# Softmax minus one-hot over 8192 columns: half of the loads and stores of X issued on Pool's queue in place of SP's

## The chip, the cores and the metric

The kernel runs on one core of a Trainium2 chip. The metric is device time in microseconds (us), the median of three runs; lower is better. The engines are named as in the profile: DVE is VectorE, ACT is ScalarE, POOL is GpSimd (called Pool here), SP is SyncE, which does nothing but issue transfers, and PE is TensorE.

## What is computed

The reference takes logits of shape 8 x 1024 x 8192 in fp32 and one integer label for each of the 8192 rows. For each row it computes the softmax and subtracts 1 at the label's column:

```
logits_max = np.max(logits, axis=-1, keepdims=True)
exp_logits = np.exp(logits - logits_max)
softmax = exp_logits / np.sum(exp_logits, axis=-1, keepdims=True)
one_hot[batch_idx, seq_idx, labels] = 1.0
return (softmax - one_hot).astype(np.float32)
```

268 MB are read and 268 MB are written.

## The kernel before

**Blocks and slots.** The 8192 rows are cut into B = 32 blocks of 256 rows. A block lies in SBUF as 128 partitions with G = 2 rows each (j = 0 and 1), so that partition p holds 64 KB that are contiguous in HBM. The tile X has SLOTS = 3 such blocks, and block b uses slot b % 3. Everything is done in place: a block is loaded into X, computed on in X, and stored from X. Block b + 3 can be loaded only when block b has been stored.

**Pieces.** Each load and each store of a block is made in two pieces of 4.19 MB, q = 0 and 1. PIECES (line 105) knows two ways to cut. In "r", piece q is row j = q of all 128 partitions. In "h", piece q is both rows of the even (q = 0) or the odd (q = 1) partitions. LOADS and STORES (lines 13 and 14) say which cut each block uses: blocks 0 to 3 and 31 are loaded by rows, the others by halves; block b is stored as block b + 3 is loaded. So a load's piece q overlaps only the piece q of the store before it in the same slot.

**Order of the transfers.** `transfers` (lines 139 to 144) is written out by hand: the six loads of blocks 0 to 2, and then for each block b its two stores and the two loads of block b + 3. All are issued on SP's queue in this order. `run` (line 63) records an instruction; where it must wait for a semaphore, the engine that issues it waits, and whatever stands behind it on that engine waits too. `load` (line 120) waits for the store of the same piece three blocks earlier to have landed (semaphores `put`). The load of block 2's second row waits for `w_iota`, since the iota is made in that place of X first. `store` (line 130) waits for the VectorE instruction that finishes the piece's last row: for a store by halves that is row 1 of the block, for both halves.

**Compute.** For each of the 64 row tiles (128 x 8192): VectorE takes the negated maximum (`row_max`, line 155, TENSOR_REDUCE), ScalarE computes exp with the row's sum, VectorE takes the reciprocal, ScalarE scales by it, and VectorE computes x - (iota == label) (SCALAR_TENSOR_TENSOR). On VectorE the maximum of row tile t + 1 stands ahead of the last step of row tile t. The iota lies in PSUM as int16. It is made once, on Pool (line 86), and copied to PSUM by VectorE (line 98). The maximum of a row tile waits for all pieces that hold a part of it: by halves, for both loads of the block.

**Pool** makes an identity for the transpose of the labels, then the iota, and after that has nothing to do. All instructions go through `run`, so the profile gives line 68 for nearly all of them; they are told apart by tile and operation. Line 198 is SP's wait for the last stores.

Of the kernel before, what the change touches and what calls it, by code (L numbers as in the profile page):

```python
# [8 lines left out]
G = 2  # L9
SLOTS = 3  # L10
# [7 lines left out]
def kernel(  # L18
# [6 lines left out]
    nc = tc.nc  # L25
# [30 lines left out]
    with tc.tile_critical():  # L56
        sem = tc.alloc_semaphore
        got = [[sem(f"got{i}{q}") for q in range(2)] for i in range(SLOTS)]
        put = [[sem(f"put{i}{q}") for q in range(2)] for i in range(SLOTS)]
# [3 lines left out]
        def run(engine, waits, counter, method, **operands):  # L63

            waits = list(dict.fromkeys(waits))
            for w in waits[:-1]:
                engine.wait_ge(*w)  # L67
            instruction = getattr(engine, method)(**operands)  # L68
            for w in waits[-1:]:
                instruction._wait_ge(*w)  # L70
            step = 16 if method == "dma_start" else 1
            instruction.then_inc(counter, step)
            count[counter.name] = count.get(counter.name, 0) + step
            return counter, count[counter.name]
# [3 lines left out]
        w = run(nc.gpsimd, [], pool, "memset", ap=ident[:], constant=0.0)  # L78
# [13 lines left out]
        for j in range(G):  # L92
            w = run(
                nc.tensor, [w_ident, w_lab], pe, "transpose",
                out=lab_ps[:, j, :], in_=lab_f[:, j, :], identity=ident[:],
            )
# [14 lines left out]
        def meets(a, b):  # L111

            sets = [[set(range(*d.indices(n))) for d, n in zip(p, (P, G))] for p in (a, b)]
            return all(x & y for x, y in zip(*sets))


        loaded, stored, finished = {}, {}, []
        last_made = [((every, slice(G - 1, G)), w_iota)]

        def load(b, q):  # L120
            piece = PIECES[LOADS[b]][q]
            ps, js = piece
            before = stored.get(b - SLOTS, last_made if b == SLOTS - 1 else [])
            w = run(
                nc.sync, [w for other, w in before if meets(piece, other)], got[b % SLOTS][q],
                "dma_start", out=X[ps, b % SLOTS, js, :], in_=x_b[b, ps, js, :],
            )
            loaded.setdefault(b, []).append((piece, w))

        def store(b, q):  # L130
            piece = PIECES[STORES[b]][q]
            ps, js = piece
            w = run(
                nc.sync, [finished[b * G + js.stop - 1]], put[b % SLOTS][q],
                "dma_start", out=o_b[b, ps, js, :], in_=X[ps, b % SLOTS, js, :],
            )
            stored.setdefault(b, []).append((piece, w))

        transfers = [(load, b, q) for b in range(SLOTS) for q in range(G)]
        for b in range(B):  # L140
            transfers += [(store, b, q) for q in range(G)]
            if b + SLOTS < B:
                transfers += [(load, b + SLOTS, q) for q in range(G)]
# [23 lines left out]
        for t in range(T):  # L167
            x = row(t)
            label = lab[:, t % G, t // G : t // G + 1]
            w = run(  # L170
                nc.scalar, [w_max], act, "activation",
                out=x, in_=x, func=Act.Exp, bias=m[:, t : t + 1], scale=1.0, accum_out=s[:, t : t + 1],
            )
# [13 lines left out]
            for c, w in zip(cols, scaled):  # L187
                w = run(
                    nc.vector, [w], dve, "scalar_tensor_tensor",
                    out=x[:, c], in0=iota[:, c], scalar=label, in1=x[:, c],  # L190
                    op0=Alu.is_equal, op1=Alu.subtract, reverse1=True,
                )
# [36 lines left out]
```

## Time and profile before

| | |
|---|---|
| median of 3 runs | 1251.36 us (1250.57 to 1251.69) |
| the profiled execution | 1251.85 us |
| its span in the profile | 1250.1 us |
| DVE busy | 1116.5 us (89%) |
| ACT busy | 919.0 us (74%) |
| POOL busy | 7.4 us (1%) |
| moved | 536.99 MB, 430 GB/s over the span |
| issues of X on SP's queue | 64 loads, 64 stores |
| median from issue to landing, by halves | 19.3 us a load, 28.9 us a store |

The rows of the page that name an operation read: line, engine, operation, output<-input, shapes, count, busy us in all, mean ns of one, then the engine's idle time just ahead of them and what ended it. A DMA queue's row gives packets, MB, and the time of its packets as a share of 16 engines' span. In the chain and in the timeline the first number is the start and the second the duration, both in us from the start of the span; "x2" is two instructions merged into one row, so that its duration includes what lies between them. SPq is SP issuing a transfer; the transfer itself goes on long after the issue has ended, until its landing, when the last of its bytes is reported by semaphore.

### The profile page before, as it was taken

The page shows a single profiled execution, that of the slowest core. Times are in us where ns is not written, and L with a number is a line of the kernel's source. Part 1 is how long each engine was busy: PE and PEld are TensorE (multiplying, and loading weights), DVE is VectorE, ACT ScalarE, POOL GpSimd, SP SyncE. Part 2 cuts the span into 40 slices and gives each one's busy share as a digit, 9 for nine tenths or more (in the row PEclk, how much of TensorE's full clock was granted, in tenths as well). Part 3 has the DMA queues.
Part 4 walks back from the last instruction along what each step waited for, and adds up shares of the span by engine and source line. Part 5 has one row for each costly group of instructions (what it writes and reads, how often), then busy time and mean ns, then how long its engine had stood idle before and what let it go on. Part 6 is the DMA issues. An engine that isn't in the chain of part 4 may idle for free.

```text
span 1250.1 us, 646 instructions
## 1 busy us (share of the span) xinstructions
PE 0.4 (0%) x2; PEld 0.3 (0%) x2; DVE 1116.5 (89%) x196; ACT 919.0 (74%) x194; POOL 7.4 (1%) x7
## 2 busy tenths in 40 slices
PE   0000000000000000000000000000000000000000
PEld 0000000000000000000000000000000000000000
DVE  5999999988899888998888988889888898888993
ACT  3888888777777777777778777687767877778782
POOL 2000000000000000000000000000000000000000
DMA  9999999999999999999999999999999999999998
GB/s 405 419 432 424 432 434 436 434 430 424 428 430 436 436 432 436 434 432 436 436 436 434 432 432 430 430 428 436 432 436 436 436 436 436 434 436 419 447 417 350
DMA packets 11317, 536.99 MB, mean 430 GB/s; under 512 B 2064, under 2 KB 2064, under 8 KB 2096
## 3 DMA queue, kind: packets, MB, share of 16 engines
q1 hardware_dynamic: 11264, 536.88, 99.6%
q10 hardware_dynamic: 48, 0.07, 0.0%
q14 instruction: 5, 0.04, 0.0%
HBM read 268.50 MB, written 268.44 MB: 430 GB/s over the span
## 4 chain that ended last, share of the span: by engine, by line
DMA 74%; DVE 21%; SPq 2%; ACT 1%; issue 1%; PE 0%; ACTq 0%; DVEq 0%
DMA out_dram<-X 72%; DVE m L68 10%; DVE X L68 10%; SPq L68 2%; DMA X<-in_logits_dram 2%; ACT X L68 1%; DMA lab_raw<-in_labels_dram 1%; DVE iota L68 0%; DVE r L68 0%; DVE lab_f L68 0%; PE iota L68 0%; DVE lab L68 0%; ACTq L224 0%; DVEq L67 0%; SPq L56 0%
## 5 line engine op out<-in xcount | busy, mean ns | idle before, releaser
L68 DVE TENSOR_REDUCE m<-X 128x1 f32<-128x8192 f32 x64 | 555.2, 8675 | 98.3 <-DMA X<-in_logits_dram 98.3
L68 ACT ACTIVATE X<-X,m 128x8192 f32<-128x8192 f32 x64 | 455.8, 7122 | 212.6 <-DVE m L68 212.6
L68 DVE SCALAR_TENSOR_TENSOR X<-iota,lab,X 128x8192 f32<-128x8192 int16 (+1 forms) x65 | 559.6, 8611 | 3.8 <-ACT X L68 3.8
L68 ACT ACTIVATE X<-X,r 128x8192 f32<-128x8192 f32 (+1 forms) x65 | 456.0, 7017 | 95.6 <-DVE r L68 95.6
L68 DVE RECIPROCAL r<-s 128x1 f32<-128x1 f32 x64 | 9.8, 154 | 7.3 <-ACT X L68 7.3
L68 ACT ACTIVATION_READ_ACCUMULATOR X<-X,m 128x1 f32 x64 | 11.9, 186 | 0.0
L68 DVE CAST lab_f<-lab_raw 32x256 f32<-32x256 int32 x1 | 1.0, 993 | 7.4 <-DMA lab_raw<-in_labels_dram 7.4
L68 POOL IOTA X<- 128x8192 int16 x1 | 6.9, 6943 | 0.0
L68 DVE TENSOR_SCALAR iota<-X 128x4096 int32<-128x4096 int32 x1 | 4.4, 4427 | 0.1
L68 ACT ACT_TABLE_LOAD x1 | 1.3, 1283 | 1.4 <-SPq L56 1.4
L68 DVE COPY lab<-iota 128x64 f32<-128x64 f32 x1 | 0.2, 225 | 0.5 <-PE iota L68 0.5
L68 PE MATMUL iota<-ident,lab_f 32*128 32x32 f32 x2 | 0.4, 302 | 8.5 <-DVE lab_f L68 8.5
L68 PEld LDWEIGHTS iota<-ident,lab_f 32*128 32x128 f32 x2 | 0.3, 196 | 8.4 <-DVE lab_f L68 8.4
L68 POOL TENSOR_SCALAR_AFFINE_SELECT ident<-ident 32x32 f32<-32x32 f32 x1 | 0.2, 202 | 0.1
L68 POOL MEMSET ident<- 32x32 f32 x1 | 0.1, 114 | 0.5 <-SPq L56 0.5
L213 POOL MEMSET const-bfloat16-1.0<- 128x1 bf16 x1 | 0.1, 106 | 0.0
L213 POOL MEMSET const-uint8-127<- 128x1 uint8 x1 | 0.1, 106 | 0.0
L213 POOL MEMSET const-float32-0.0<- 128x1 f32 x1 | 0.1, 103 | 0.2 <-issue 0.2
L213 POOL MEMSET const-float32-1.0<- 128x1 f32 x1 | 0.1, 103 | 0.0
## 6 DMA issues: line engine op xcount, KB each, us to landing
X<-in_logits_dram SPq DMA_DIRECT2D x10, 4096.0 KB, 20.6
out_dram<-X SPq DMA_DIRECT2D x6, 4096.0 KB, 21.9
out_dram<-X SPq DMA_DIRECT2D x58, 28.9
X<-in_logits_dram SPq DMA_DIRECT2D x54, 19.3
lab_raw<-in_labels_dram ACTq DMA_DIRECT2D x1, 64.0 KB, 6.5
```

The lines of the kernel that those rows point to most:

```text
L68: instruction = getattr(engine, method)(**operands)
L213: nc = _bacc.Bacc("TRN2", target_bir_lowering=False, num_devices=1)
```

## The change

A list of the two issuing engines is added, and each load and store takes its engine from it by its piece number q:

```
         loaded, stored, finished = {}, {}, []
+        ring = [nc.sync, nc.gpsimd]
...
             w = run(
-                nc.sync, [w for other, w in before if meets(piece, other)], got[b % SLOTS][q],
+                ring[q], [w for other, w in before if meets(piece, other)], got[b % SLOTS][q],
                 "dma_start", out=X[ps, b % SLOTS, js, :], in_=x_b[b, ps, js, :],
             )
...
             w = run(
-                nc.sync, [finished[b * G + js.stop - 1]], put[b % SLOTS][q],
+                ring[q], [finished[b * G + js.stop - 1]], put[b % SLOTS][q],
                 "dma_start", out=o_b[b, ps, js, :], in_=X[ps, b % SLOTS, js, :],
             )
```

Piece 0 (row 0, or the even partitions) stays on SP's queue, and piece 1 (row 1, or the odd partitions) goes to Pool's queue. Each of the two queues keeps the order of its own pieces; between the two there is no order but the semaphores that were there before. The slots, the pieces, the waits and all instructions of the other engines stay. The wait for the last stores stays on SP.

More of the change, by code (lines that the diff above doesn't have):

```diff
@@ L117 @@
         loaded, stored, finished = {}, {}, []
+        ring = [nc.sync, nc.gpsimd]
         last_made = [((every, slice(G - 1, G)), w_iota)]
@@ L124, in load @@
             w = run(
-                nc.sync, [w for other, w in before if meets(piece, other)], got[b % SLOTS][q],
+                ring[q], [w for other, w in before if meets(piece, other)], got[b % SLOTS][q],
                 "dma_start", out=X[ps, b % SLOTS, js, :], in_=x_b[b, ps, js, :],
@@ L133, in store @@
             w = run(
-                nc.sync, [finished[b * G + js.stop - 1]], put[b % SLOTS][q],
+                ring[q], [finished[b * G + js.stop - 1]], put[b % SLOTS][q],
                 "dma_start", out=o_b[b, ps, js, :], in_=X[ps, b % SLOTS, js, :],
```

## The prediction

> **What bounds the kernel now.** I read the page first: busy shares, the DMA rows, the chain's shares, the costliest groups.
>
> ```profile
> PE 0.4 (0%) x2; PEld 0.3 (0%) x2; DVE 1116.5 (89%) x196; ACT 919.0 (74%) x194; POOL 7.4 (1%) x7
> ...
> q1 hardware_dynamic: 11264, 536.88, 99.6%
> ...
> DMA 74%; DVE 21%; SPq 2%; ACT 1%; issue 1%; PE 0%; ACTq 0%; DVEq 0%
> ...
> L68 DVE TENSOR_REDUCE m<-X 128x1 f32<-128x8192 f32 x64 | 555.2, 8675 | 98.3 <-DMA X<-in_logits_dram 98.3
> ```
>
> The 16 DMA engines are the bound: one queue, q1, which is SP's, keeps them busy 99.6% of the span, and VectorE's idle time ahead of the row maximum is all put down to loads. Pool is almost unused. Then the chain of waits in order of time, at the last steady blocks and the end:
>
> ```profile
> 1056.46 37.44 DMA out_dram<-X
> 1094.47 0.60 SPq L68
> 1095.11 37.43 DMA out_dram<-X
> 1132.55 19.28 DMA X<-in_logits_dram
> 1151.86 8.69 DVE m L68
> ```
>
> (The short rows of issue lie between them.) One store follows another at 1095.11 - 1056.46 = 38.65 us. A block moves four pieces of 4.19 MB, two loads and two stores, so one piece takes **D = 9.66 us**, and all 128 take 1237 us of the 1250.1 us span. From 1151.86 on, the chain is VectorE's to the end. Third, SP's own queue in the timeline, which shows how the order covers its waits:
>
> ```profile
> 1094.47 1.23 SPq L68 DMA_DIRECT2D out_dram<-X  x2
> 1122.90 10.16 SPq L68 DMA_DIRECT2D X<-in_logits_dram  x2
> 1133.11 1.06 SPq L68 DMA_DIRECT2D out_dram<-X  x2
> ```
>
> Two stores are issued; 28.4 us later the first has landed and SP issues the first load; the second store lands 10 us later, then the second load and at once the next two stores. While SP waits for the first store, the second is still moving. That is why the engines never run dry. Last, the view of the tile X and the start of the timeline:
>
> ```profile
> L68 SPq DMA_DIRECT2D X<-in_logits_dram x64: 328/507/531, 1.0 to 1171.3; - x64
> L68 SPq DMA_DIRECT2D out_dram<-X x64: 343/595/802, 47.0 to 1233.9; - x64
> DMA to landing us min/median/max: 12.4/20.7/49.4
> ```
>
> ```profile
> 0.96 13.07 SPq L68 DMA_DIRECT2D X<-in_logits_dram  x6
> 1.31 6.94 POOL L68 IOTA X<- 128x8192 int16 x1
> 13.58 8.68 DVE L68 TENSOR_REDUCE m<-X 128x1 f32<-128x8192 f32 x1
> ```
>
> The quickest transfer needs 12.4 us from issue to landing and 9.66 of them are data, so a queue that has run dry loses **G = 2.8 us** between the last byte of one transfer and the first byte of the next (issue, way out, way back of the semaphore; I take half of it on either side).
>
> **The change part by part.** In the built program the lists of TensorE, VectorE and ScalarE are the same. Of SP's 128 transfers of X, 64 go to Pool, behind its iota, in the same order. Nothing is removed: the bytes are the same, and q1 is already at 99.6%, so the data terms cannot shrink. SP's issue time (0.5 to 0.6 us each) was hidden and is worth nothing. What changes is **what covers a wait**. Each queue now runs store, wait for its landing, load, next store. A load waits behind a store of its own queue, and only the other queue can cover these 2.8 us.
>
> Take both queues to share the engines evenly. If both stores of a block start together, they land together, and each block leaves the engines idle for 2.8 us. If Pool's queue has w us of work left when SP's store lands, only 2.8 - w is idle. They do start together: at 98.91 SP issues both stores of block 1 within 1.2 us, because one VectorE result releases both. From then on w changes per block by the difference in turnaround between the two queues, **d**.
>
> d is not in this trace. Pool issues no DMA there. The nearest rows are SP's issues, 0.33 to 0.80 us; below, Pool could save such an issue (d = -0.5, which makes SP the lagging queue at the same price); above, the longest Pool row is the iota, 6.9 us, far from anything like an issue. I take **d = 0.6**, one more SP issue.
>
> - Start. Pool's loads begin behind the iota, which ends at 1.31 + 6.94 = 8.25, so with 1.4 + 0.6 their data from 10.25. Row 0's load, alone so far, has about 1.8 us left (landed about 13.4, less 1.4) and takes twice that. The row maximum, at 13.58 just behind it, comes **1.7 us** later, and VectorE is the chain until 203 us.
> - Early blocks. 2.8 - 0.6n for n = 1 to 4: 2.2 + 1.6 + 1.0 + 0.4 = **5.2 us**.
> - Middle. With w between 2.8 and about one piece, nothing is idle.
> - Late blocks. w cannot grow past a piece: a store needs the row after its block to have been reduced (order of VectorE), so it is ready 8.67 + 8.74 = 17.4 us after both halves of the next block's load. Then SP's queue waits for Pool's load through VectorE, is empty itself, and Pool's own turnaround is bare. From about 16 blocks of 0.6 on (block 18), some 13 blocks lose between 0 and 2.8 each. I take 0.6, what Pool lags by each time: **8 us**.
> - End. Before, the last waited-for load landed at 1151.84; the VectorE chain from there to the last store's issue (1233.9) is 82.1, and a transfer at least 12.4, in all 94.5; the ten pieces left then were 96.6. The two are nearly even. If Pool's half of that load comes w = 9 us later while SP works ahead, the chain sets the end: 9 - 2.1 = **6.9 us**.
>
> Sum 1.7 + 5.2 + 8 + 6.9 = 21.8 us. The profiled execution took 1251.85 (span 1250.1 and 1.75 around it); with the sum 1273.7. The median shown is 0.5 lower, 1251.36; so **1273 us**, +1.7%. The last three terms all have the cover as their reason: without any of it they would be 81 us.
>
> VectorE's large instructions all run at one rate: 8192 elements in 8675 ns (maximum) and 8742 ns (last step), 4096 in 4427 ns (copy of the iota), 1.06 to 1.08 ns each; none shows a faster mode. The Trainium skill, SBUF — State Buffer, "SBUF: two separate sides", warns against exactly this move: while VectorE holds the port pair that it shares with GpSimd in a two-port mode, GpSimd can't write descriptors, and Pool's DMAs starve. Its condition is not met by these rows as I read them; were it met, each Pool issue could wait one VectorE instruction, an estimate of up to 8.7 us x 29 blocks = 252 us. The same skill, DMA: Bandwidth & Descriptors, "Issuing engines are not separate DMA queues", says that several issuers save sequencer time only; by it alone the sum would be 0. No run here shows either for Pool.
>
> **Rivals.**
> 1. *A bare turnaround in every block.* Two ways lead there: d about 0, so that the queues stay in step; or the engines do not share evenly between the queues, so that the favoured one always finishes, waits for VectorE, and leaves the other's turnaround uncovered. 29 loads wait for a store: 29 x 2.8 = 81 us, 1332; with the longer turnaround of 3.4, 99 us, 1350. For it: both stores of a block have one releaser. Against it: any steady difference d takes the queues apart.
> 2. *All covered.* If one queue lags from the first by 3 to 9 us (Pool's loads start 7.3 us after SP's) and stays so, the start's 1.7 and an end between 0 and 3 remain, and the late start may be hidden: 1250 to 1255. Against it: the common release at 98.9 puts them in step.
> 3. *Faster.* Not every block takes 38.65 us: from 241.23 to 785.91 the chain's 14 blocks take 38.91 on average, 3.6 us too many in all. If that is one queue held up at its head, a second queue passes it, and with rival 2's cover the time is 1251.4 - 3.6 = 1247.8. It decides only if w stays within 3 to 9 and the start costs nothing.
> 4. *Pool's issues are held up* by several us each (d towards 6.9): a turnaround of 9.7 in most blocks, up to 281 us.
>
> **How the numbers follow.** Forecast 0.55, with its own range 1255 to 1310 (d from 0.2 to 2: more in the early term at the low end, more late blocks at the high end); rival 1 0.23 (1310 to 1350); rival 4 0.03; rival 2 0.12, of which 0.02 are above 1253.9; rival 3 0.07. A measurement of this kernel tells about 0.2% (2.5 us) from no change. Faster 0.07; within 0.2% 0.10; slower 0.83. The range 1252 to 1345 leaves out rival 3, most of rival 2 and rival 4, under 0.2 together.
>
> **What would show it.** Right: two queues of 268 MB each; the DMA share under 99% in the slices behind 100 us and towards the end; chain periods above 38.65 by 0.5 to 2; the same durations on VectorE and ScalarE; Pool's landings behind SP's by a growing distance. Wrong: equal GB/s in every slice (rivals 2, 3); each period at 41.4 or more (rival 1); Pool's issues many times SP's 0.5 us, or packets on Pool's queue of another size than the 64 KB rows (uneven shares); a piece that takes longer than 9.66 us with both queues full, which nothing above allows for.

## The result and the profile after

The changed kernel takes **1358.3 us** (median of 4 runs, 1354.02 to 1365.82) against 1251.44 before (4 runs): 1.086 times as long, 95% interval 1.081 to 1.092. It is slower by 107 us, where 22 were forecast. The profiled execution took 1354.67 us with a span of 1352.9. Of all runs below, one counts as slow, the 1319.2 us of the kernel with Pool made later once: the ratios leave it out, the medians and ranges do not.

The page of the changed kernel, lines on engines, DMA queues and groups:

```profile
PE 0.4 (0%) x2; PEld 0.3 (0%) x2; DVE 1117.0 (83%) x196; ACT 919.0 (68%) x194; POOL 41.4 (3%) x71
...
q0 software_dynamic: 5632, 268.44, 48.3%
q1 hardware_dynamic: 5632, 268.44, 47.6%
...
L68 DVE TENSOR_REDUCE m<-X 128x1 f32<-128x8192 f32 x64 | 555.3, 8676 | 197.2 <-DMA X<-in_logits_dram 197.2
```

VectorE and ScalarE do what they did, in the same time; VectorE only waits 99 us longer for loads. The two queues carry half each, in the same number of packets, but the shares do not add up to the old ones. Packets took 48.3 + 47.6 = 95.9% of 1352.9, that is 1297 us, against 99.6% of 1250.1 = 1245 us. The engines were without a packet for 55 us, against 5. So **the loss has two halves: 50 us of idle engines, and 52 us in which the same packets took longer.** The prediction had a term for the first only.

Where in time: the chain of waits in the middle of the changed kernel.

```profile
588.11 41.74 DMA out_dram<-X
629.85 0.28 issue
630.13 0.53 POOL X L68
630.66 41.66 DMA out_dram<-X
672.31 0.28 issue
672.60 0.53 POOL X L68
673.12 41.96 DMA out_dram<-X
```

A block now takes 673.12 - 630.66 = 42.5 us in place of 38.65, 3.8 us too many; by the landings of SP's stores, blocks 2 to 26 take 42.4 us on average (40.7 to 43.5). And the two issuing queues over the same two blocks, in the timelines of SP and of Pool (start, duration):

```profile
627.45 0.49 SPq L68 DMA_DIRECT2D X<-in_logits_dram  x1
630.34 0.49 SPq L68 DMA_DIRECT2D out_dram<-X  x1
669.94 0.49 SPq L68 DMA_DIRECT2D X<-in_logits_dram  x1
672.82 0.49 SPq L68 DMA_DIRECT2D out_dram<-X  x1
```

```profile
630.13 0.53 POOL L68 DMA_DIRECT2D X<-in_logits_dram  x1 [41.49 <-DMA out_dram<-X]
630.66 0.53 POOL L68 DMA_DIRECT2D out_dram<-X  x1
672.60 0.53 POOL L68 DMA_DIRECT2D X<-in_logits_dram  x1 [41.41 <-DMA out_dram<-X]
673.12 0.53 POOL L68 DMA_DIRECT2D out_dram<-X  x1
```

SP's store lands and SP issues its load (627.45, 669.94); Pool issues its own 2.7 us later, both times. The landings of the two stores are 2.4 us apart, and stay so in every block from 2 to 26. One packet of 64 KB takes 2.42 us: the two queues run in step, one packet apart.

The packets of the trace show why this lag covers so little. A piece by halves is four packets of 64 KB on each of the 16 engines and then, on each, a packet of four bytes that reports the engine as done; a piece has landed with the last of the 16 reports. Around 627 us, 14 engines end their last store packet, one of Pool's, between 626.6 and 627.5. SP's store lands at 627.43, and the first packet of SP's load starts at 628.73. In between, these engines have nothing to move. SP learns of its landing so late for two reasons. On these 14 engines its own last packet had ended by 622.7, but each report came only behind one more packet of Pool's, 2.4 us later; in the whole run 987 of the 1024 reports of SP's queue stand right behind a packet of Pool's. And the other two engines report still later, at 626.85 and 627.07, while SP waits for all 16.

### The profile page after: what moved, and what is told of

Read it like the earlier page. It is cut to its first block, busy times and chain, and to the rows that moved or that the text cites. A ratio compares the mean times of both kernels' runs of the same rounds, so it can differ in the third digit from the quotient of the medians.

```text
span 1352.9 us, 646 instructions
## 1 busy us (share of the span) xinstructions
PE 0.4 (0%) x2; PEld 0.3 (0%) x2; DVE 1117.0 (83%) x196; ACT 919.0 (68%) x194; POOL 41.4 (3%) x71
## 3 DMA queue, kind: packets, MB, share of 16 engines
q0 software_dynamic: 5632, 268.44, 48.3%
q1 hardware_dynamic: 5632, 268.44, 47.6%
## 4 chain that ended last, share of the span: by engine, by line
DMA 77%; DVE 19%; issue 1%; POOL 1%; ACT 0%; SPq 0%; POOLq 0%
DMA out_dram<-X 64%; DMA X<-in_logits_dram 13%; DVE m L68 10%; DVE X L68 10%; POOL X L68 1%; ACT X L68 0%; DVE r L68 0%; POOL out_dram L68 0%; SPq L68 0%; POOL ident L68 0%; POOLq L68 0%; POOLq L225 0%; SPq L56 0%
## 5 line engine op out<-in xcount | busy, mean ns | idle before, releaser
L68 POOL DMA_DIRECT2D X<-in_logits_dram x32 | 17.2, 536 | 1135.9 <-DMA out_dram<-X 1131.4
L68 POOL DMA_DIRECT2D out_dram<-X x32 | 17.0, 530 | 155.8 <-DVE r L68 125.9
```

## The experiments

Theories. **Cover**: a load that waits for its store's landing costs nothing as long as another transfer is in flight, and the change took that transfer away. **Mixing**: two queues on one engine lengthen each other's packets. **Software**: Pool's queue is slow by itself. Later, for the forecast's own failed step: **drift** (a longer turnaround on one queue takes the queues apart) against lockstep. The kernel before was timed again in each group, 1251.7 to 1251.8 us.

| kernel | median us (range) | ratio to before, 95% | packets, us | idle, us |
|---|---|---|---|---|
| before | 1251.4 | | 1245 | 5 |
| the change | 1358.3 (1354.0 to 1365.8) | 1.081 to 1.092 | 1297 | 55 |
| all on Pool's queue | 1269.8 (1269.2 to 1270.6) | 1.013 to 1.016 | 1246 | 23 |
| loads SP, stores Pool | 1291.5 (1287.8 to 1299.2) | 1.028 to 1.037 | 1275 | 15 |
| only odd loads on Pool | 1259.4 (1255.6 to 1264.3) | 1.004 to 1.008 | 1252 | 6 |
| only odd stores on Pool | 1415.1 (1413.3 to 1418.6) | 1.129 to 1.133 | 1319 | 93 |
| quarters, two queues | 1267.7 (1266.4 to 1269.1) | 1.011 to 1.014 | 1250 | 18 |
| quarters, one queue | 1260.1 (1258.4 to 1260.7) | 1.005 to 1.009 | 1248 | 9 |
| whole blocks, one queue | 1350.9 (1350.2 to 1352.2) | 1.078 to 1.081 | 1290 | 58 |
| whole blocks, store after load | 1362.2 (1361.5 to 1363.2) | 1.087 to 1.090 | 1262 | 98 |
| change, Pool 1 us later each block | 1351.0 (1347.5 to 1352.6) | 1.077 to 1.081 | 1291 | 55 |
| change, Pool 3.9 us later each block | 1388.5 (1387.0 to 1391.0) | 1.107 to 1.111 | 1293 | 96 |
| change, Pool 7.8 us later once | 1295.3 (1284.6 to 1319.2) | 1.025 to 1.039 | 1278 | 23 |

"Packets" is the queues' share times the span of the profiled execution, "idle" the rest of that span. Experiments start from the changed kernel.

### All on Pool's queue

```diff
-        ring = [nc.sync, nc.gpsimd]
+        ring = [nc.gpsimd, nc.gpsimd]
```

> All loads and stores of X on Pool's queue, in the order that SP's had. Cover theory (the change costs because a load's wait for its store is no longer covered by another transfer of the same queue): the cover is whole again, 1250 to 1258 us, no idle engines, packets of 64 KB at 2.42 us. Mixing theory (two queues on one engine lengthen each other's packets): one queue alone, so the same 1250 to 1258. Software theory (Pool's queue is itself slow): over 1300 us, more than the change's own 1358, with long packets or gaps on queue q0.

Measured 1269.8 us. The packets take what they took before (1246 us), and from 400 to 1100 us the trace has 432.9 GB/s, against 433.6 in the kernel before. So **Pool's queue is not slow**: the software theory falls. The 18 us lie at the two ends, and the expectation missed them. Pool's first load stands behind the iota, at 8.2 us in place of 0.96. And the view of SP's waits has a row that the kernel before lacks:

```profile
SPq L56 <- POOLq L56: 10.3, 1, 10.3
```

At the end of the program, after the last store has landed, SP waits 10.3 us for Pool. The changed kernel has 5.1 us in this row, and the runs with 32 DMAs on Pool 2.5: 0.08 us for each DMA that Pool has issued (10.3 / 128, 5.1 / 64, 2.5 / 32).

### Loads on SP's queue, stores on Pool's

```diff
-                ring[q], [w for other, w in before if meets(piece, other)], got[b % SLOTS][q],
+                nc.sync, [w for other, w in before if meets(piece, other)], got[b % SLOTS][q],
...
-                ring[q], [finished[b * G + js.stop - 1]], put[b % SLOTS][q],
+                nc.gpsimd, [finished[b * G + js.stop - 1]], put[b % SLOTS][q],
```

> All loads on SP's queue, all stores on Pool's, so that loads of one block and stores of another run side by side on every engine. Cover theory: the two stores of a block follow each other in one queue, the second covers the first one's landing: no idle engines, 1252 to 1262 us. Mixing theory: two queues side by side nearly all the time, packets longer than 2.42 us by as much as in the change or more: 1300 us and above. Software theory: about half of what all on Pool's queue loses.

Measured 1291.5 us, between the two. The idle time does go (15 us, 5.1 of them at the end), as the cover theory said; but packets still take 30 us more than before, though less than in the change. So longer packets do not come from idle time alone; what lengthens them here, where no queue goes from loads to stores by itself, was not found.

### Only the odd loads, and only the odd stores, on Pool's queue

The change cut in two. In the first, `store` goes back to `nc.sync`; in the second, `load` does.

> Half of the change: only the loads of piece 1 go to Pool's queue; all stores stay on SP's, one behind the other. Cover theory: the second store covers the first one's landing and the first load covers the second's: 1252 to 1262 us, DMA share at 99% again. Mixing theory: two queues side by side during the loads, about half of the lengthening of packets stays, some 25 us: 1275 to 1285. Software theory: a quarter of the bytes on Pool's queue, 1275 or more.

> The other half of the change: only the stores of piece 1 go to Pool's queue; all loads stay on SP's. Both stores of a block now move side by side and land together. Cover theory: both loads wait for landings with nothing else in flight, the idle time of the change (about 50 us) comes back whole: 1300 to 1360 us, and far from the run with only the odd loads moved. Mixing theory: like the run with the odd loads moved, 1275 to 1285. Software theory: like that run too.

Measured **1259.4 us** with the odd loads moved and **1415.1 us** with the odd stores moved. The first runs two queues side by side during the loads and loses 8 us, 2.5 of them the wait for Pool at the end. The second has as many DMAs on Pool as the first and is slower than the whole change. The mixing theory had the two alike; it falls as the cause of the loss. The cover theory had their order and the first within its range; the second is beyond its 1360, and why it costs 57 us more than the whole change is not shown. SP's and Pool's queues in that run, from the two timelines:

```profile
745.30 1.11 SPq L68 DMA_DIRECT2D X<-in_logits_dram  x2
753.04 0.50 SPq L68 DMA_DIRECT2D out_dram<-X  x1
790.65 1.11 SPq L68 DMA_DIRECT2D X<-in_logits_dram  x2
```

```profile
753.30 0.54 POOL L68 DMA_DIRECT2D out_dram<-X  x1 [45.06 <-DVE r L68]
```

Both loads are issued together, at the landing of SP's one store, and 45 us pass to the next time. SP's store stands behind two loads, Pool's does not. In most blocks Pool's store lands 9.5 us ahead of SP's, which then moves alone, and nothing covers its landing.

### Quarters: the change with cover inside each queue

```diff
-            "r": [(every, slice(j, j + 1)) for j in range(G)],
-            "h": [(slice(i, P, 2), rows) for i in range(2)],
+            "r": [(slice(i, P, 2), slice(j, j + 1)) for i in range(2) for j in range(G)],
+            "h": [(slice(i, P, 4), rows) for i in range(4)],
...
-        ring = [nc.sync, nc.gpsimd]
+        ring = [nc.sync, nc.gpsimd] * 2
```

(With four semaphores a slot and four pieces in `transfers`; the control has `[nc.sync] * 4`.)

> The change kept, but every piece cut in two (by halves: partitions 0, 4, 8.. and 2, 6, 10.. on SP's queue, 1, 5, 9.. and 3, 7, 11.. on Pool's), so that each queue has a second store in flight while it waits for its first to land. Cover theory: the idle time goes and with it most of the lengthening of packets: 1252 to 1270 us, most of the change's loss undone with both queues still carrying half each. Mixing theory: two queues side by side as before and twice the boundaries between transfers: 1310 us or more, whatever the idle time does.

> Control for the run with quarters on two queues: the same quarters in the same order, all on SP's queue. All theories: 1249 to 1256 us, as before; over 1265 would say that cutting the pieces costs something by itself, which must then be taken off the two-queue run.

Measured 1267.7 us on two queues and 1260.1 on one. Each queue now has a second store in flight while it waits for the first, and 91 of the 107 us are gone, as the cover theory had it, with both queues still carrying half of every block. From 400 to 1100 us the trace has 432.7 GB/s on two queues and 433.3 on one. The 7.5 us between them are less than the 10.3 that SP waits for Pool at the end (128 DMAs again). The control missed its 1256 by 4: cutting the pieces costs some 8 us, at the two ends.

### Whole blocks on one queue: the bare turnaround alone

```diff
-LOADS = "rrrr" + 27 * "h" + "r"
-STORES = "r" + 27 * "h" + "r" + "hh" + "r"
+LOADS = "rrrr" + 27 * "w" + "r"
+STORES = "r" + 27 * "w" + "r" + "hh" + "r"
...
-        ring = [nc.sync, nc.gpsimd]
+        ring = [nc.sync, nc.sync]
```

("w" is the whole block in one piece, and `transfers` counts the pieces of each cut. Loads are whole for blocks 4 to 30, not from block 1.)

> One queue (SP's), blocks 1 to 30 moved by loads, and blocks 1 to 27 by stores, in one piece of 8.4 MB: a load waits for a store with nothing else in flight, and no second queue exists. Cover theory: the bare turnaround shows alone: at least 27 x 2.8 = 76 us, with the wait for the slowest of the 16 engines up to 130: 1325 to 1385 us, engines idle at every load; if the restart itself lengthens packets, they are longer than 2.42 us here too. Mixing theory: only idle time, no packet longer than in the kernel before, and at most 1330 us.

Measured 1350.9 us: **the loss of the change, without Pool and without a second queue**, in both halves, 58 us idle and packets of 1290 us. Its page and its chain of waits (rows of issue left out):

```profile
q1 hardware_dynamic: 10400, 536.88, 95.7%
```

```profile
631.24 41.79 DMA out_dram<-X
673.04 0.33 SPq L68
673.41 42.43 DMA out_dram<-X
```

673.41 - 631.24 = 42.2 us a block, the change's 42.5. A queue that has to wait for its own store with nothing behind it is enough. In the trace the longer packets are the same two of a load's eight on each engine: the first, after the gap (about 3.1 us in place of 2.42), and the last, with the next store right behind it (mostly 3.3 to 4.1). The changed kernel has them in other places: in its block at 628 us, the first two packets of an engine take 3.3 and 2.9 us on average and the one at the switch from loads to stores 3.0.

### The same, with each store kept until the load ahead has landed

```diff
-                ring[q], [finished[b * G + js.stop - 1]], put[b % SLOTS][q],
+                ring[q], [w for _, w in loaded.get(b + SLOTS - 1, [])] + [finished[b * G + js.stop - 1]], put[b % SLOTS][q],
```

> The run with whole blocks on one queue, and in addition each store waits until the load ahead of it in the queue has landed, so that the engines never go from a load straight to a store. It asks where the longer packets come from. In the whole-block run the packets' time was 95.7% of 1348.4 us, 1290 us, 52 above the 1238 that they would take at 2.42 us per 64 KB. Restart theory (packets are long where all 16 engines begin at the same moment after a gap): two restarts in each block, so the packets take as long or longer, 1290 us and up, and the time is 1351 + 27 x 2.8 and a little more, 1425 to 1460. Switch theory (they are long where the engines go from loads to stores without a gap): the part at the switch goes, packets' time 1250 to 1270, and the time 1351 + 76 less 30, 1385 to 1410.

Measured: 1362.2 us, with packets 92.8% of 1359.7 = 1262 us, as the switch theory had it. In the trace the load's last packet is back at 2.42 us and only the first stays long; a store's first packet after a gap takes 2.45. So the 3.8 us that a bare turnaround costs per block in the whole-block run have three parts: about 2 us with no packet, 0.7 in the first packets of a load, and 1.1 where all engines go from loads to stores at once. The time came out below the 1385 expected: the second gap costs about 1.5 us a block ((98 - 58) / 27), not 2.8, and a store after a gap has no long packet. Why a switch lengthens the last packet is open. In the whole-block run the 16 engines begin that packet within 1.1 us of each other. In the kernel before they drift apart, until the first and the last to report a store are 5.7 us apart, and the long packet goes: at 137 us they begin it within 1.1 us and all 16 are long (3.6 us on average), at 178 us within 1.3 us and three are, and later never more than six. But the run with all on Pool's queue has 16 long ones from 958 to 960 us, though its engines report that load up to 6.2 us apart; so the spread is not shown to be the reason. No run was made to try the spread by itself.

### The forecast's step: Pool made later on purpose

```diff
+            waits = [w for other, w in before if meets(piece, other)]
+            if q == 1 and b >= SLOTS:
+                for _ in range(1):
+                    waits = [run(nc.gpsimd, waits, pool, "iota", out=late[:], pattern=[[1, 1024]], base=0, channel_multiplier=0)]
...
```

The two other runs have `range(4)`, and `b == 8` with `range(8)`. One such iota takes 0.97 us.

> The change, and ahead of each of Pool's 29 waiting loads, once its store has landed, one iota of 1024 columns on Pool into a tile that nothing reads (about 0.9 us): Pool's turnaround is made longer than SP's on purpose, by the d that the prediction assumed (0.6) and half as much again. The prediction's step (a steady difference d pulls the two queues apart until one covers the other): faster than the change despite the added work, 1275 to 1300 us. Lockstep theory (the queues are brought back in step in every block, whatever d is): each block pays the delay too, 1358 + 29 x 0.9 = 1384.

> The same with four such iotas ahead of each of Pool's waiting loads, about 3.6 us. The prediction's step: apart after two or three blocks, but the lag reaches its limit early and Pool's long turnaround is bare in the later blocks: 1280 to 1310 us. Lockstep theory: 1358 + 29 x 3.6 = 1462.

> The change, with eight such iotas (about 7.2 us) ahead of one of Pool's loads only, that of block 8: the queues are moved apart once. If the lag then stays (no force towards lockstep): the blocks after it lose little and the time is 1265 to 1290. If the queues fall back in step within a few blocks: 1355 to 1370, as the change.

With 0.97 us added per block: 1351.0, 7 us less than the change, at the edge of the noise (the two intervals just meet), though 28 us of work were added. It is neither expectation. The drift is there: the landings of the two stores of a block are 2.4 us apart up to block 4, then 7.2, 12.1, 16.5, 17.1, 21.8 and 25.9 at block 10, and in between the periods fall to 36.7. Then the lag stays between 22 and 26, and 14 blocks from 605.0 to 1199.3 (SP's landings) take 42.5 us each on average. At its limit the loss of a bare turnaround is back in full. The timelines of SP and of Pool there:

```profile
648.84 0.49 SPq L69 DMA_DIRECT2D X<-in_logits_dram  x1
673.49 0.49 SPq L69 DMA_DIRECT2D out_dram<-X  x1
```

```profile
673.23 0.97 POOL L69 IOTA late<- 128x1024 int16 x1 [39.95 <-DMA out_dram<-X]
674.49 0.54 POOL L69 DMA_DIRECT2D X<-in_logits_dram  x1 [0.29 <-POOL late L69]
```

SP's store is issued only 25 us after its load, held by the result of VectorE, and just then Pool's own store lands. With 3.9 us the limit is reached by block 4, and the time is 1388.5, again neither expectation.

Moved apart once, by 7.8 us: **1295.3 us, 63 less than the change** (four runs, 1284.6, 1287.8, 1302.8 and 1319.2; the median without the last is 1287.8, inside the expected 1265 to 1290). The lag jumps to 16.9, settles at 12.1 and stays within 1 us of it for twenty blocks; nothing pulls the queues back into step. The idle time falls from 55 to 23 us. Packets stay long (1278); that this is because in each block one queue still goes from a load to a store while the other loads is not shown.

## Why the prediction was wrong

- **What bounds the kernel**: right. DMA engines before and after; nothing changed on the compute engines.
- **That the cover of a wait is what changes**: right, and shown from both sides. Quarters give the cover back and 91 of 107 us with it; whole blocks on one queue take it away and cost 99.
- **d = 0.6 takes the queues apart: the step that failed.** Pool's issue takes 0.53 us, SP's 0.49, and Pool starts it 0.28 us after a landing (the chain's rows of issue), SP 0.02 (627.43 to 627.45). So d was about 0.3, within the 0.2 to 2 that the text allowed, and the lag did not grow even by that: 2.4 us in every block from 2 to 26. It moves in steps of about 4.8 us, two packets (2.4, 7.2, 12.1, 17.1, 21.8 in the run with 0.97 added). Each engine takes one 64 KB packet from either queue in turn (between 634 and 644 us, 14 of the 16 packets that start together are of one queue, 2.42 us later 14 are of the other), and a difference of 0.3 is not enough to move one; that this is what holds the lag is argued from these steps. The case that I gave 0.23, a loss in every block, is what happened, but neither of the ways that it named led there: d was not 0, and the engines shared evenly.
- **That a lag of w leaves only 2.8 - w idle**: wrong too. With w = 2.4 this would be 0.4 us a block, some 12 in all; the idle time grew by 50 us, 1.7 in each of 29 blocks. The rule has no term for a landing that is reported behind the other queue's packet and by the last of 16 engines.
- **The price of a bare turnaround**: 2.8 us forecast, 3.85 measured per block (42.5 - 38.65). The 2.8 was read from the quickest issue to landing, but that transfer, a store of block 1 issued at 98.91, stood behind a load whose packets ran until 101, so it shows no queue that has run dry. That the first load of all, on an empty queue, took 12.5 us (0.96 to 13.46) makes the figure right by luck. A term for packets longer than 2.42 us was missing, some 52 us in all; the text had named this as what nothing in it allowed for. That is why 1358 lies above the rival's 1332 and 1350. The stated range ended at 1345, inside that rival's own 1310 to 1350.
- **Late blocks, 0.6 us each**: wrong as well. In the run that does drift, the limit costs 42.5 - 38.65 = 3.85 in each block, not 0.6, and the time is 78 us above the forecast. Nor is the middle free: with a lag that stays at 12.1 us, a little over one piece, blocks 9 to 27 take 40.0 us each on average.
- **Start, 1.7 us**: right in size. The first stores of block 1 are issued at 100.91 in place of 98.91, 2.0 later; but only 1.0 of it is the load of row 0 (14.61 in place of 13.58), the rest is the wait for Pool's load of row 1, which lands at 31.58.
- **End, 6.9 us**: another reason. The lag that it was made of never came; 5.1 us are SP's wait for Pool after the last landing, which no row of the trace before could show.
- **VectorE's port**: no starving of Pool is to be seen. With all transfers on Pool's queue the steady rate is 432.9 GB/s beside the same VectorE instructions. That was the reading of the rows, against the warning of the Trainium skill (SBUF — State Buffer, "SBUF: two separate sides"), whose condition, a two-port mode, I read these instructions not to meet; the longest of Pool's 64 issues took 0.67 us, none a VectorE instruction's 8.7. Its other statement, that several issuers only save sequencer time (DMA: Bandwidth & Descriptors, "Issuing engines are not separate DMA queues"), is true of the bandwidth here and says nothing of the 107 us.

## What to carry to other kernels

When transfers are spread over queues, ask of each wait on a landing what is still in flight while it lasts: two pieces that cover each other in one queue lose this when they start side by side, for then they also land side by side. A split is safe where the pieces that wait, and not those waited for, go to the other queue (1259 against 1415 us), or where each queue keeps a second transfer of its own behind the first (quarters, 1268). A lag between two queues should not be counted on to build up by itself: here it did not in 25 blocks, and one push of 7.8 us lasted for twenty.

## What was not expected of the hardware

- Pool's queue moves data at SP's rate: 432.9 against 433.6 GB/s in the middle of the run.
- The end of the program waits 0.08 us for each DMA that Pool has issued: 2.5, 5.1 and 10.3 us for 32, 64 and 128.
- In the whole-block runs, the first 64 KB packet of a load after a gap takes about 3.1 us, and the last one ahead of a store without a gap mostly 3.3 to 4.1, in place of 2.42. A store's first packet after a gap takes 2.45.
- With two queues, the report of a landing waits its turn too: in the changed kernel, 987 of the 1024 four-byte packets that report SP's transfers stand right behind a packet of Pool's.
- The 16 engines report one transfer's end up to 5.7 us apart in the kernel before, with the full 433.6 GB/s in those blocks.
